# Retention's queries computed with channels on partitions, and the rotation tables moved: one change to a two-layer hybrid decoder kernel

## Chip, cores and metric

The kernel runs on one core of a Trainium2 chip. The metric is the device time of one execution in microseconds (us), as the median of several runs. A trace of one further execution shows when each engine was busy: PE (matmul), PEld (its weight loads), DVE (vector), ACT (scalar), POOL (GpSimd), and SP, which only issues DMAs here.

## The reference

Two layers of a decoder trunk over 1024 tokens and 1024 channels. Each layer norms and modulates its input, projects it to 3088 columns, and runs three groups of heads on them: attention over a window of 128, retention, and gated linear attention (GLA). Their outputs, gated, go through one output projection. Retention is what the change touches:

```python
rq = apply_rotary(rq.reshape(B, S, RET_HEADS, RET_DK), positions, ret_freq)
rk = apply_rotary(rk.reshape(B, S, RET_HEADS, RET_DK), positions, ret_freq)
r = retention(rq, rk, rv)          # 4 heads of 64, chunks of 128 tokens
# in a chunk: sc = (q k^T) * decay(i - j);  out = sc v + (q * q_decay) state
#             state = chunk_decay * state + (k * k_decay)^T v
r_out = rms_norm(r) * silu(rg)
```

`apply_rotary` multiplies the two halves x1 and x2 of each head by cosines and sines of position times frequency: (x1 cos - x2 sin, x2 cos + x1 sin). Attention and retention have different frequencies, so there are two sets of tables.

## The kernel before, in words

**Tiles.** Tokens stand in 8 tiles of 128, taken in pairs p = 0 to 3. The normed and transposed input of a pair, `hT`, holds channels on partitions, as a high and a low part; weights are split alike when they are loaded (ACT or DVE makes the high part, DVE or POOL the low part, L533). A projection of one tile is 24 products of 128x256: three combinations of parts over 8 slices of channels. `project` has the tokens as the stationary side, so its result has tokens on partitions; `project_T` has the weights as the stationary side, so its result has channels on partitions, and serves 512 tokens at once. Results go to three PSUM banks in turn (`mm`), everything else to five (`aux`).

**The order of the work.** PE's order is the order in which the program is written, and it is written with a clock: every matmul adds its estimated time to `clk`, jobs (Python generators) say how long to wait before their next step (the numbers in the table `L`), and after every 7 products `pump` runs the steps that are due. A flag with a delay does the same for a result that others await. So a number in `L` moves a step of a job between the products of a projection, on PE and, through the scheduler that follows program order, on the other engines. All DMAs but a few are issued by SP, in order: a DMA whose source isn't ready holds those behind it.

**Retention** (in `layer`, from L1500 on). For each pair the queries, keys and values of two tiles are projected, tokens on partitions. `ret_rot` rotates queries and keys on DVE with five instructions (`rotary`, L823 to L828) and multiplies them by a decay per token and head (L1157: `qdec`, `kdec`). Values are copied by ACT. `ret_core` then transposes queries and keys of a tile with four PE transposes into one bank, copies the bank to SBUF (ACT, 512 columns), makes scores of keys and queries (4 products of 64 rows, two banks), masks them on DVE (L1179), and multiplies them with the values and the state; DVE updates the state (L1198, L1200). The output is normed per head and gated (L973 to L979).

**Tables.** `tables` computes the sines and cosines of all tokens on DVE and ACT, tokens on partitions (L414 to L442, `sincos`). Retention uses them as they are. Attention has its queries with channels on partitions; for it `tables_T` repeats the sines over heads (DVE, L449), transposes (four PE transposes for each of 4 pairs), copies and stores to DRAM (`tabS`, L458), and `attn_rot` loads them back with 16 DMAs (L864).

**Banks and weights.** While a bank of `mm` is read by DVE or ACT, two more projections can run; the third needs it again. Weights of later units are loaded through 5 staging buffers (`st`) that they share with the modulation weights of the next layer; those are multiplied and summed on DVE (L364).

Of the kernel before, what the change touches and what calls it, by code (L numbers as in the profile page):

```python
# [60 lines left out]
def host_constants():  # L61
# [12 lines left out]
    c["qdec"] = (gam[None, :] ** (i[:, None] + 1.0)).astype(f)  # L74
    c["kdec"] = (0.125 * gam[None, :] ** (-(i[:, None] + 1.0))).astype(f)
# [18 lines left out]
def trunk(ctx: ExitStack, tc: tile.TileContext, ins, cst, out):  # L94
# [168 lines left out]
    tabS = dr.tile([NP_, P, 2, 256], F32, name="tabS")  # L263
# [147 lines left out]
    def tables():  # L411
        PIF = float(np.nextafter(np.float32(math.pi), np.float32(0)))
        ang = t2()
        V.tensor_tensor(ang.rearrange("p (t k) -> p t k", t=NT), posf.unsqueeze(2).to_broadcast((P, NT, 64)),  # L414
                        freq.unsqueeze(1).to_broadcast((P, NT, 64)), ALU.mult)
        yield
        nn = t2()
# [7 lines left out]
        n2 = t2()  # L425
# [4 lines left out]
        red = t2()  # L430
# [13 lines left out]
    def tables_T():  # L444

        for p in range(NP_):
            yield L["tt1"]
            rep_ = t2()
            V.tensor_copy(rep_.rearrange("p (s t h k) -> p s t h k", s=2, t=2, h=4),  # L449
                          sincos[:, 2 * p:2 * p + 2, :, 0:32].rearrange("p t s k -> p s t k").unsqueeze(3)  # L450
                          .to_broadcast((P, 2, 2, 4, 32)))
# [179 lines left out]

    def rstd_of(ss, w, scale, eps):
        r = small(w)
        V.tensor_scalar(r, ss, scale, eps, ALU.mult, ALU.add)  # L634
# [133 lines left out]
    qdec = cload("qdec")  # L768
    kdec = cload("kdec")
# [89 lines left out]
    def attn_rot(l, hf, g, w_):  # L859
# [3 lines left out]
        for s, d in ((0, sn), (1, cs)):  # L863
            nc.sync.dma_start(d.rearrange("p (s n) -> p s n", s=2),  # L864
                              tabS[2 * hf:2 * hf + 2, :, s, :].rearrange("s p n -> p s n"))
# [288 lines left out]
    def ret_rot(t, src, dec_):  # L1154
        r = t1()
        rotary(r, src, 4, t, 1)
        eng("rdec").tensor_tensor(h4(r), h4(r), dec_.unsqueeze(2).to_broadcast((P, 4, 64)), ALU.mult)  # L1157
# [564 lines left out]
```

## Time and profile before

| | before |
|---|---|
| median of 3 runs | 998.0 us (997.8 to 999.6) |
| the profiled execution's own time | 996.3 us |
| its span, first to last instruction | 994.6 us |
| instructions | 19641 |
| PE, DVE, ACT, POOL busy | 965.7, 683.2, 409.3, 246.3 us |
| retention, layer 1 and layer 2 | about 93 to 206 us and 593 to 677 us |
| PE's clock, mean | 0.991 of full |

The span is divided into busy time and idle time of each engine. Matmuls overlap: a product's time from start to end is longer than the distance between the starts of two neighbours, and it is the distance that adds up. The tables of groups name an engine's instructions by source line, output, input and shape; the last part of a group's row is the time for which the engine stood idle before them, and what it then waited for.

### The profile page before, as it was taken

The page shows a single profiled execution, that of the slowest core. Times are in us where ns is not written, and L with a number is a line of the kernel's source. Part 1 is how long each engine was busy: PE and PEld are TensorE (multiplying, and loading weights), DVE is VectorE, ACT ScalarE, POOL GpSimd, SP SyncE. Part 2 cuts the span into 40 slices and gives each one's busy share as a digit, 9 for nine tenths or more (in the row PEclk, how much of TensorE's full clock was granted, in tenths as well). Part 3 has the DMA queues.
Part 4 walks back from the last instruction along what each step waited for, and adds up shares of the span by engine and source line. Part 5 has one row for each costly group of instructions (what it writes and reads, how often), then busy time and mean ns, then how long its engine had stood idle before and what let it go on. Part 6 is the DMA issues. An engine that isn't in the chain of part 4 may idle for free.

```text
span 994.6 us, 19641 instructions
## 1 busy us (share of the span) xinstructions
PE 965.7 (97%) x7133; PEld 824.3 (83%) x7133; DVE 683.2 (69%) x1679; ACT 409.3 (41%) x1152; POOL 246.3 (25%) x310
## 2 busy tenths in 40 slices
PE   5899999999999999999999999999999999999996
PEld 1599999888998777778889999988999877777785
DVE  3779857677766777664677286775766577567876
ACT  2477312233332656632555332133333257574222
POOL 2322001233310234420124101113322034545000
PEclk8899999999999999999999999999999999999999
DMA  9843513523135355587555241352122434378883
GB/s 321 290 138 97 159 44 115 177 86 121 61 100 166 91 157 168 170 274 239 189 170 171 69 150 38 118 157 83 53 93 86 127 91 133 112 235 266 267 262 139
DMA packets 112305, 148.77 MB, mean 150 GB/s; under 512 B 12065, under 2 KB 63821, under 8 KB 112209
## 3 DMA queue, kind: packets, MB, share of 16 engines
q1 hardware_dynamic: 106512, 137.96, 44.5%
q10 hardware_dynamic: 5696, 9.56, 2.6%
q8 instruction: 56, 0.92, 0.4%
q14 instruction: 41, 0.33, 0.1%
HBM read 109.20 MB, written 36.18 MB: 146 GB/s over the span
## 4 chain that ended last, share of the span: by engine, by line
PE 80%; DVE 7%; DMA 7%; issue 2%; POOL 1%; ACT 1%; SPq 0%; ACTq 0%; POOLq 0%; DVEq 0%
PE mm L165 61%; PE aux L165 14%; PE aux L180 5%; DMA st<-in_w_in_dram 2%; POOL sm L635 1%; DMA t<-aoS 1%; DMA st<-in_w_last_dram 1%; DMA xk<-in_x_dram 1%; DVE arena L533 1%; DMA a<-mixS 1%; DVE t L1248 0%; DVE t L328 0%; DMA t<-in_x_dram 0%; DMA t<-xs 0%; DMA mixS<-t 0%
## 5 line engine op out<-in xcount | busy, mean ns | idle before, releaser
L165 PE MATMUL mm<-arena 128*128 128x256 f32 (+2 forms) x1824 | 299.9, 318 | 1.8 <-ACT arena L704 1.8
L165 PE MATMUL mm<-arena,arena 128*128 128x256 f32 (+2 forms) x1824 | 298.2, 316 | 0.0
L165 PEld LDWEIGHTS mm<-arena 128*128 128x128 f32 x1824 | 255.5, 191 | 26.0 <-issue 3.3
L165 PEld LDWEIGHTS mm<-arena,arena 128*128 128x128 f32 x1824 | 252.2, 188 | 24.3 <-issue 3.7
L635 POOL TENSOR_TENSOR sm<-sm,mhalf 128x1 f32<-128x1 f32 (+1 forms) x64 | 55.8, 872 | 335.9 <-DVE sm L634 317.8
L165 PE MATMUL mm<-arena,mx 128*128 128x512 f32 (+1 forms) x564 | 130.6, 387 | 0.5 <-ACT kept L1341 0.5
L165 PEld LDWEIGHTS mm<-arena,mx 128*128 128x128 f32 x564 | 101.4, 188 | 24.7 <-issue 1.9
L149 ACT ACTIVATE t<-aux 128x256 f32<-128x256 f32 (+2 forms) x124 | 55.8, 468 | 73.8 <-PE aux L180 62.2
L149 ACT ACTIVATE arena<-st 128x512 fp32r<-128x512 f32 x94 | 56.2, 627 | 53.2 <-DMA st<-in_w_in_dram 19.4
L929 POOL TENSOR_TENSOR smx<-smx,sm 128x512 f32<-128x512 f32 x32 | 36.1, 1129 | 125.7 <-DVE sm L928 118.0
L533 POOL TENSOR_TENSOR arena<-st,arena 128x512 fp32r<-128x512 f32 x31 | 42.7, 1378 | 79.7 <-ACT arena L149 72.9
L533 DVE TENSOR_TENSOR arena<-st,arena 128x512 fp32r<-128x512 f32 x77 | 58.0, 775 | 5.2 <-ACT arena L149 3.3
L925 ACT ACTIVATE smx<-smx,sm 128x129 f32<-128x129 f32 x128 | 49.9, 393 | 25.9 <-DVE sm L922 25.7
L364 DVE SCALAR_TENSOR_TENSOR acc<-st,c_act,acc 128x512 f32<-128x512 f32 x60 | 46.7, 778 | 16.9 <-DMA st<-in_w_mod_dram 16.5
L180 PE MATMUL aux<-c_ident,t 128*128 128x128 f32 (+1 forms) x292 | 48.2, 282 | 5.4 <-DVE t L666 5.0
L180 PEld LDWEIGHTS aux<-c_ident,t 128*128 128x128 f32 (+1 forms) x292 | 35.0, 144 | 12.4 <-DVE t L666 6.9
L698 ACT ACTIVATE t<-aux,mod,mod 128x128 f32<-128x128 f32 x68 | 25.9, 459 | 43.0 <-DVE t L1248 18.1
L165 PEld LDWEIGHTS aux<-t,mx 32*128 32x128 f32 (+1 forms) x896 | 39.5, 187 | 3.9 <-issue 2.1
L973 ACT ACTIVATE t<-aux 128x256 f32<-128x256 f32 x32 | 12.3, 383 | 73.6 <-PE aux L165 65.0
L165 PE MATMUL aux<-t,mx 32*128 32x32 f32 (+1 forms) x896 | 40.7, 272 | 0.0
L920 DVE COPY_PREDICATED smx<-c_curmask,aux 128x256 f32<-128x256 int32 x64 | 25.4, 446 | 19.5 <-ACT smx L149 17.2
L1248 DVE SCALAR_TENSOR_TENSOR t<-t,sm,t 128x512 f32<-128x512 f32 x32 | 24.0, 780 | 18.2 <-DMA t<-in_x_dram 10.8
(224 smaller groups left out, 1387.7 us busy)
## 6 DMA issues: line engine op xcount, KB each, us to landing
st<-in_w_in_dram SPq DMA_DIRECT2D x96, 256.0 KB, 3.8
st<-in_w_mod_dram SPq DMA_DIRECT2D x64, 256.0 KB, 3.1
mx<-mixS SPq DMA_DIRECT2D x20, 512.0 KB, 4.9
mixS<-t SPq DMA_DIRECT2D x72, 128.0 KB, 3.7
st<-in_w_last_dram SPq DMA_DIRECT2D x36, 256.0 KB, 3.8
wm<-in_w_mod_dram SPq DMA_DIRECT2D x12, 512.0 KB, 7.0
t<-in_x_dram SPq DMA_DIRECT2D x24, 256.0 KB, 4.9
t<-tabS SPq DMA_DIRECT2D x16, 256.0 KB, 4.6
```

What stands on the lines that cost most here:

```text
L149: A.activation(dst, src, AF.Copy)
L165: T.matmul(dst, lhsT, rhs, start=start, stop=stop)
L180: T.transpose(dst, src, idn)
L364: V.scalar_tensor_tensor(acc, wt, c_act[:, k:k + 1], acc, ALU.mult, ALU.add)
L533: e.tensor_tensor(lo, st, f(hi), ALU.subtract)
L635: G.tensor_tensor(r, r, mhalf[:, :w], ALU.pow)
L698: A.activation(hf[:, ks], at[kt], AF.Identity, scale=gain, bias=shift)
L920: V.copy_predicated(sv, curmask.unsqueeze(1).to_broadcast((P, 2, P)), pv[:, :, n // P - 1, :])
L925: A.activation(sm[:, h, :], sm[:, h, :], AF.Exp, bias=mx[:, h:h + 1], accum_out=sums[:, h:h + 1])
L929: eng("pn").tensor_tensor(sm[:, :, 0:128], sm[:, :, 0:128], rs.unsqueeze(2).to_broadcast((P, 4, P)), ALU.mult)
L973: A.activation(sq, po, AF.Square)
L1248: V.scalar_tensor_tensor(xt[j], yg[j], r, xt[j], ALU.mult, ALU.add)
```

## The change

**Queries.** `ret_q` projects the queries of a pair with the weights as the stationary side, 2 x 24 products of 128x256 into one bank, channels on partitions, and rotates them there with six DVE instructions on 512 columns: four partial products with the sines, each on 32 partitions and written to the neighbouring 32, one product with the cosines, one sum. Queries are kept for the pair in `rq`, and need no transposes. A group of 32 partitions is one half of one head.

**Decays.** They leave queries and keys. Values are multiplied by `vdec` on DVE, straight from PSUM, instead of being copied by ACT; the query's factor is left out, since the norm per head removes it, but for its constant: `reps` has a value per token and head.

**Tables.** `sincos` is transposed as it is, 8 PE transposes in all. The two halves are stored to `tabS`; four loads put retention's part into SBUF for good (`tab`, one copy for each group of 32 partitions), and 16 stores of 32 partitions write attention's part, once for each of 4 heads, to `tabA`, from which `attn_rot` loads. The computation of the tables uses a large buffer in place of small ones and is due earlier (`tb1` 12.59 instead of 24.5), and the first queries await the flag `tab`.

**Copies and masks.** The copy of the transposed keys (256 columns now) and the masking of scores are put at high priority for the scheduler.

**Delays.** Some 40 numbers of `L` are changed, and four are new.

```diff
+    tabS = dr.tile([2, 2, 32, S], F32, name="tabS")
+    tabA = dr.tile([4, 32, 2, S], F32, name="tabA")
+    tab = cp.tile([P, 2, S], F32, name="tab")
...
     def tables_T():
-        for p in range(NP_):
-            yield L["tt1"]
-            rep_ = t2()
-            V.tensor_copy(rep_..., sincos[:, 2 * p:2 * p + 2, :, 0:32]...)
-            yield L["tt2"]
+        for i in range(2):
+            yield L["tt1"] if i == 0 else L["tt2"]
             pt = aux()
-            for i in range(4):
-                transp(pt[:, i * P:(i + 1) * P], rep_[:, i * P:(i + 1) * P], ident)
+            for t in range(4):
+                transp(pt[:, t * P:(t + 1) * P], sincos[:, 4 * i + t].rearrange("p s k -> p (s k)"), ident)
             tb = t2()
             A.activation(tb, pt, AF.Copy, scale=0.125)
-            nc.sync.dma_start(tabS[p], tb.rearrange("p (s n) -> p s n", s=2))
+            ts = slice(512 * i, 512 * i + 512)
+            nc.sync.dma_start(tabS[:, :, :, ts].rearrange("s c k n -> (s c k) n"), tb)
+            tbs.append(tb)
+        yield L["tt3"]
+        for b in range(4):
+            nc.sync.dma_start(tab[32 * b:32 * b + 32], tabS[:, 1].rearrange("s k n -> k s n"))
+        flag("tab", L["tt6"])
+        for i in range(2):
+            for h in range(4):
+                yield L["tt4"]
+                for j in range(2):
+                    nc.sync.dma_start(tabA[h, :, j, 512 * i:512 * i + 512], tbs[i][64 * j:64 * j + 32])
...
+    def project_P(pm, l, p, w, c):
+        h = hT[(l, p)]
+        accum(pm, lambda a, k: w[:, a, k, c:c + P], lambda b, k: h[:, b, k, 0:256])
...
+    def ret_q(l, p, w):
+        pm = mm()
+        for c in range(2):
+            project_P(pm[:, 256 * c:256 * c + 256], l, p, w, c * P)
...
+        for b in range(4):
+            r = slice(32 * b, 32 * b + 32)
+            o = two(x)[32 * (b ^ 1):32 * (b ^ 1) + 32]
+            if b % 2:
+                V.scalar_tensor_tensor(o, two(pm)[r], -1.0, sn[r], ALU.mult, ALU.mult)
+            else:
+                V.tensor_tensor(o, two(pm)[r], sn[r], ALU.mult)
+        V.tensor_tensor(two(u), two(pm), cs, ALU.mult)
...
+        V.tensor_tensor(q, u, x, ALU.add)
+        flag(("rq", l, p), L["rq1"])
...
     def ret_core(l, t, q, k, v):
...
         for j in range(2):
-            transp(pt[:, j * P:(j + 1) * P], q[:, j * P:(j + 1) * P], ident)
-            transp(pt[:, (2 + j) * P:(3 + j) * P], k[:, j * P:(j + 1) * P], ident)
-        copy("rT", tt_, pt)
+            transp(pt[:, j * P:(j + 1) * P], k[:, j * P:(j + 1) * P], ident)
+        kTt = t1()
+        with tc.high_priority():
+            copy("rT", kTt, pt[:, 0:256])
+        yield (0.0, ("rq", l, t // 2))
...
-                        copy("rv", v, src)
+                        V.tensor_tensor(h4(v), h4(src), vdec.unsqueeze(2).to_broadcast((P, 4, 64)), ALU.mult)
...
-"rc1": 0.8, "rc1@1": 0.37, "rc3@1": 1.9, "tb1": 24.5, "tb2": 0.75, "pf2": 4.16, "kv2": 2.11
+"rc1": 0.8, "rc1@1": 0.0, "rc3@1": 2.72, "tb1": 12.59, "tb2": 0.89, "pf2": 5.11, "kv2": 5.4
```

The order of instructions, at three places. PE, layer 1, from the first value projections (`mm`) of pair 0 to the first scores; before:

```order
L165 MATMUL mm_1428<-arena_320,arena_71 128x256 x24
L165 MATMUL mm_1458<-arena_320,arena_71 128x256 x7
L165 MATMUL aux_1466<-gaT_417,gwt 128x512
L180 MATMUL aux_1476<-c_ident,t_222_1281 128x128
L180 MATMUL aux_1476<-c_ident,t_234_1368 128x128
L180 MATMUL aux_1476<-c_ident,t_222_1281 128x128
L180 MATMUL aux_1476<-c_ident,t_234_1368 128x128
L165 MATMUL mm_1458<-arena_320,arena_71 128x256 x14
L165 MATMUL aux_1497<-t_251_1481 128x128
```

And in the changed kernel, where `rq` holds the queries and t_241 the transposed keys:

```order
L165 MATMUL mm_1433<-arena_322,arena_71 128x256 x24
L165 MATMUL mm_1463<-arena_322,arena_71 128x256 x14
L180 MATMUL aux_1478<-c_ident,t_230_1385 128x128 x2
L165 MATMUL mm_1463<-arena_322,arena_71 128x256 x7
L165 MATMUL aux_1490<-gaT_419,gwt 128x512
L165 MATMUL mm_1463<-arena_322,arena_71 128x256 x3
L165 MATMUL aux_1508<-rq_1345,t_241_1481 128x128
```

Two transposes of keys are left of four, and 10 products with a gate's product stand between them and the scores, where 14 did.

DVE, the same place, from the first rotation on; before, the first query rotation (`mm_1206`) and what follows it:

```order
L823 TENSOR_TENSOR t_222_1281<-mm_1206,sincos 128x256
L1066 TENSOR_TENSOR gs_1249<-gs_1249,t_216_1235 128x2
L825 TENSOR_TENSOR tr_1282<-mm_1206,sincos 128x4x32
L826 TENSOR_TENSOR tr_1282<-mm_1206,sincos 128x4x32
L827 TENSOR_TENSOR t_222_1281<-t_222_1281,tr_1282 128x4x32
L828 TENSOR_TENSOR t_222_1281<-t_222_1281,tr_1282 128x4x32
L449 COPY t_237_1384<-sincos 128x512
L1157 TENSOR_TENSOR t_222_1281<-t_222_1281,c_qdec 128x256
```

In the changed kernel the query product of the pair is `mm_1231`, the first key product `mm_1351`:

```order
L1184 TENSOR_TENSOR t_224_1339<-mm_1231,tab 32x512
L1182 SCALAR_TENSOR_TENSOR t_224_1339<-mm_1231,tab 32x512
L1184 TENSOR_TENSOR t_224_1339<-mm_1231,tab 32x512
L838 TENSOR_TENSOR t_230_1385<-mm_1351,sincos 128x256
L840 TENSOR_TENSOR tr_1386<-mm_1351,sincos 128x4x32
L841 TENSOR_TENSOR tr_1386<-mm_1351,sincos 128x4x32
L1182 SCALAR_TENSOR_TENSOR t_224_1339<-mm_1231,tab 32x512
L1185 TENSOR_TENSOR t_223_1338<-mm_1231,tab 128x512
```

Three more of this rotation and the five of the second key tile follow, and behind these the value weights (`st` of L154, as `arena_322`), with the modulation's (`acc`) between them:

```order
L843 TENSOR_TENSOR t_234_1424<-t_234_1424,tr_1425 128x4x32
L541 TENSOR_TENSOR arena_322<-st_1321,arena_322 128x512
L366 SCALAR_TENSOR_TENSOR acc_1244<-st_1332,c_act,acc_1244 128x512
L541 TENSOR_TENSOR arena_322<-st_1349,arena_322 128x512
L366 SCALAR_TENSOR_TENSOR acc_1244<-st_1402,c_act,acc_1244 128x512
```

The six instructions of a pair's rotation replace ten and two decays of the two tiles, and the low parts of the value weights come after the second key rotation.

SP, between the stores of gates (`sgS`, `srS`) at the end of layer 1's gate projections, in the changed kernel; before, no table was handled here:

```order
L460 DMA tab<-tabS 32x2x1024
L154 DMA sgS<-t_191_1111 128x256
L460 DMA tab<-tabS 32x2x1024 x3
L154 DMA sgS<-t_197_1155 128x256
L154 DMA srS<-t_202_1191 128x256
L466 DMA tabA<-t_178_1047 32x512 x2
L154 DMA srS<-t_206_1227 128x256
L466 DMA tabA<-t_183_1085 32x512 x4
L154 DMA st_1321<-in_w_in_dram 128x512
L466 DMA tabA<-t_183_1085 32x512 x2
```

The loads of `tab` and ten of the small stores stand between the gates' stores and the value weights.

More of the change, by code (lines that the diff above doesn't have):

```diff
@@ L1500, in layer @@
         G.memset(stR, 0.0)
-        await_flag("tables")
+        await_flag("tab")
         for p in range(NP_):
             last = p == NP_ - 1
-            rr = {}
-            for name in ("rq", "rk", "rv"):
+            q = ret_q(l, p, used(l, "rq"))
+            pump()
+            if last:
+                load(l, "gqk")
+            ks = {}
+            for name in ("rk", "rv"):
                 w = used(l, name)
```

71 lines of the change are left out of this document (38 added, 33 removed).

## The prediction

> **What bounds the kernel now.** I read the page's engine line and slices first, then the table by stretches for the two places where retention runs, then the tensor engine's waits, and last its timeline for the price of one transpose.
>
> ```profile
> PE 965.7 (97%) x7133; PEld 824.3 (83%) x7133; DVE 683.2 (69%) x1679; ACT 409.3 (41%) x1152; POOL 246.3 (25%) x310
> PE   5899999999999999999999999999999999999996
> PE 80%; DVE 7%; DMA 7%; issue 2%; POOL 1%; ACT 1%; SPq 0%; ACTq 0%; POOLq 0%; DVEq 0%
> 93.00:206.00 113.00, 111.71 (x908) 106.39 (x908) 80.08 (x232) 31.22 (x67) 18.39 (x18) 1.00 0.40 122
> 593.00:677.00 84.00, 81.58 (x671) 77.50 (x670) 56.30 (x167) 21.27 (x45) 12.03 (x12) 1.00 0.34 105
> ```
>
> PE is busy nearly everywhere between the first and the last slice, and it is 80% of the chain that ended last. In the two stretches of retention (columns: length, busy time of PE, weight loads, DVE, ACT, POOL, then PE's clock) it is short of full by 1.3 and 2.4 us; DVE has 71% and 67%. So an instruction less on PE there is time less, if nothing else becomes late. What PE waits for there:
>
> ```profile
> PE aux L165 <- ACT t L149: 3.0, 3, 1.3
> PE aux L165 <- DVE t L1179: 0.4, 1, 0.4
> PE aux L165 <- DVE stR L1200: 0.3, 1, 0.3
> 192.83 0.71 PE L165 MATMUL aux<-t 64*128 64x128 f32 x8 [1.29 <-ACT t L149]
> 669.66 0.71 PE L165 MATMUL aux<-t 64*128 64x128 f32 x8 [1.22 <-ACT t L149]
> ```
>
> The 3.0 us are score products that wait for ACT's copy of the transposed queries and keys; with the two other rows it is 3.7 us, the whole of what these stretches wait.
>
> **Term 1: transposes go.** In each of 16 retention tiles (8 per layer) four transposes become two, and the tables need 8 instead of 16.
>
> ```profile
> 158.69 0.38 PE L180 MATMUL aux<-c_ident,t 128*128 128x128 f32 x2
> 158.83 3.11 PE L165 MATMUL mm<-arena 128*128 128x256 f32 x24
> 161.78 0.60 PE L180 MATMUL aux<-c_ident,t 128*128 128x128 f32 x4
> 162.13 2.28 PE L165 MATMUL mm<-arena 128*128 128x256 f32 x17
> L180 PE MATMUL aux<-c_ident,t 128*128 128x128 f32 x288 | 47.5, 283 | 5.4 <-DVE t L666 5.0 <-DVE mx L1121 0.2
> ```
>
> From start to start, a block of two holds PE for 0.14 us (158.69 to 158.83) and one of four for 0.35 (161.78 to 162.13): 0.21 for the two that go. 16 x 0.21 = 3.4, and two blocks of four for the tables are 0.7: **-4.1 us**. The group's mean of 283 ns is the time of one from start to end, and neighbours overlap; by it the 40 would be 11.3 us, the far end. The query product itself keeps its size: 48 products of 128x256 for two tiles before and after, only with the weights as the stationary side, as the rest of the kernel already has it in other stages.
>
> The Trainium skill, page "TensorE: Matmul & The Clock Gate", section "Part 4: PE-mode transpose", gives about 275 ns for a transpose inside a kernel; by that figure the 40 would be worth an estimated 11 us, against 4.1 by the starts. The trace has that number as the mean of one, 283 ns, and not as the spacing.
>
> **Term 2: the copy that PE waits for is halved.**
>
> ```profile
> L149 ACT ACTIVATE t<-aux 128x512 f32<-128x512 f32 x48 | 28.6, 595 | 25.7 <-PE aux L180 22.4 <-DVE t L1602 2.5 <-issue 0.4
> L149 ACT ACTIVATE t<-aux 128x256 f32<-128x256 f32 x44 | 16.8, 382 | 26.0 <-PE aux L180 17.6 <-PE aux L165 7.0 <-POOL arena L533 1.3
> ```
>
> 595 ns become 382, so the three waits lose 0.2 us each, 0.6 to 0.7. ACT also loses the 16 copies of values (one is moved to DVE below). The copy is put at high priority, but in the new order of ACT a conversion of weights, which waits for its DMA, still stands one or two instructions ahead of it at the last tile of each layer, so I don't credit the whole 3.0 us. Between 0 and -3.0 I take **-0.7**.
>
> **Term 3: DVE pays for the new form.** Old and new prices come from these rows.
>
> ```profile
> 599.48 0.41 DVE L823 TENSOR_TENSOR t<-mm,sincos 128x256 f32<-128x256 f32 x1
> 599.81 0.28 DVE L825 TENSOR_TENSOR tr<-mm,sincos 128x128 f32<-128x128 f32 x1
> 600.01 0.28 DVE L826 TENSOR_TENSOR tr<-mm,sincos 128x128 f32<-128x128 f32 x1
> L378 DVE TENSOR_TENSOR modg<-aux,st 128x512 f32<-128x512 f32 x4 | 2.7, 684 | 0.2 <-PE aux L165 0.2
> L364 DVE SCALAR_TENSOR_TENSOR acc<-st,c_act,acc 128x512 f32<-128x512 f32 x60 | 46.7, 778 | 16.9 <-DMA st<-in_w_mod_dram 16.5
> 595.97 0.57 DVE L1198 TENSOR_TENSOR stR<-stR,aux 64x128 f32<-64x128 f32 x2
> L825 DVE TENSOR_TENSOR tr<-mm,sincos 128x128 f32<-128x128 f32 x32 | 8.9, 278 | 0.0
> L1198 DVE TENSOR_TENSOR stR<-stR,aux 64x128 f32<-64x128 f32 x28 | 7.9, 281 | 0.2
> ```
>
> Rotating one tile took 0.33 + 4 x 0.20 = 1.13 us from start to start and the decay 0.33 more: for queries and keys of two tiles 4 x 1.46 = 5.8. Fewer partitions don't make an instruction shorter: 64 partitions take 281 ns (L1198) where 128 take 278 (L825). So each of the four partial multiplications, on 32 partitions of 512, costs what a whole one costs: 0.68 as a plain product, 0.78 with the sign; the cosine product and the sum are two more of 0.68. Together 4.3 us if nothing overlaps and 3.8 if each gives up the 0.08 that whole ones do. The keys (2 x 1.13) and the values (2 x 0.33, which stood on ACT) are 2.9. That is 6.7 to 7.2 for two tiles instead of 5.8, or at most 1.4 x 8 = 11 us of DVE over the kernel. In stretches where DVE has 29 to 33% free this hides; its price, if the cover were gone, is the rival "bank" below.
>
> The Trainium skill, page "VectorE: DVE Perf Modes", section "Two Vector instructions with no wait between them", says that an instruction is held until all earlier ones are finished when its start quadrant of 32 partitions differs from the last one's. By that rule the upper value, 4.3, is right, by plain overlap 3.8. The two L1198, on different halves, agree: 0.57 for two that follow each other, where L825 and L826 start 0.20 apart.
>
> **Term 4: the first queries push the value weights.** In layer 1 the second and third low part of the value weights (L541) stand in DVE's new order behind the first query rotation and both key rotations; before, they were done between the rotations. Call X the end of the first query product. A product of 24 takes 2.95 us (158.83 to 161.78), so the two key products end at X+2.95 and X+5.9, and the value product wants the second part at its 18th instruction and the third at its 20th: X+8.1 and X+8.3. DVE, in its order: three partial rotations to X+2.2, three instructions of the first key rotation from X+2.95 to X+3.7, the rest of both to X+6.2; the second key rotation to X+7.3; the second part, a 128x512 product of 0.7, to X+8.0 (in time), a weight of the modulation 0.78 (L364), the third part to X+9.5, or X+8.9 where the whole ones overlap. PE waits 0.6 to 1.2 us, once: I take **+0.9**. In layer 2 these weights stand ahead of the rotation. The bounds are 0 and 2.
>
> **Term 5: tables earlier, and out and in through DRAM.** Each is hidden, but narrowly enough to be told.
>
> ```profile
> 50.00:100.00 50.00, 50.00 (x415) 49.73 (x414) 43.73 (x106) 37.24 (x95) 12.08 (x24) 1.00 0.39 119
> 48.84 1.36 DVE L700 TENSOR_SCALAR t<-aux,mod,mod 128x128 f32<-128x128 f32 x4 [0.19 <-PE aux L180]
> 60.75 0.88 DVE L666 TENSOR_SCALAR t<-t,sm 128x512 f32<-128x512 f32 x2 [0.73 <-DMA st<-in_w_in_dram]
> 82.85 1.04 DVE L700 TENSOR_SCALAR t<-aux,mod,mod 128x128 f32<-128x128 f32 x3
> 83.86 1.04 PE L165 MATMUL mm<-arena,arena 128*128 128x272 f32 x7
> 84.41 1.28 DVE L708 TENSOR_TENSOR arena<-t,arena 128x512 fp32r<-128x512 f32 x2
> 92.27 0.43 DVE L442 TENSOR_SCALAR sincos<-sincos 128x512 f32<-128x512 f32 x1
> mixS<-t SPq DMA_DIRECT2D x16, 256.0 KB, 3.5
> t<-tabS SPq DMA_DIRECT2D x16, 256.0 KB, 4.6
> t<-t SPq DMA_DIRECT2D x32, 64.0 KB, 2.0
> ```
>
> PE now transposes the finished table just before the end of its 12th projection, which is 83.5 us in before (the 13th starts at 83.86); before, the table was ready at 92.7. DVE therefore does the 16 table instructions between the preparations of tiles 4 to 6 instead of after them. Both orders are at the same instruction at 48.84. From there to the last table instruction the new one has 20 of L700 (0.32 apart), 9 of L708 (0.60), 9 gates of 256 columns (0.33, as L823), 4 pairs of L666 (0.80), 3 weight differences and a cast (2.2), ten table instructions like L708 and six like L442 (8.1), and small ones (1.3): 29.5 us, thus 78.4 with no wait, and 82.6 if DVE rests 13% of the time, as in 50 to 100 before; I take 81, since table work fills part of the rests. PE comes at 83.5: nothing, but with 2 us in hand. Then copy 0.6, store 3.5, SP's queue and four loads (1 MB in four, 4.6 and 1.2 for the issues behind each other): 10 us, while PE has 27 instructions of 272 columns and 96 of 256 in front of the end of the first query product, some 15 us. Hidden by 5. The 16 stores of 64 KB stand on SP between weights, some 0.35 us of the queue each; the weights behind them come up to 3 us later, and are wanted later still. The 16 loads for attention keep their bytes. **0 us**, at worst +3.
>
> **The sum.** -4.1 - 0.7 + 0.9 = -3.9. The profiled execution took 996.3 us, of which 994.6 are its span; that gives 992.4. The median of the runs shown is 998.0, 1.7 above it, so I predict **994.0**.
>
> **Rivals.**
>
> *Cancelled by the start.* If DVE is some 2 us slower through the preparation of tiles 4 to 7 than I add up, PE stands at the table's transposes and again at tile 7, and every later thing shifts: 2 to 4 us, so 996 to 998. Against it is DVE's slack above; for it, that DVE's rests are few there. Chance 0.14.
>
> *Bank, the slower side.* Products go to three banks. The query product's bank is read by five DVE instructions and is wanted again after two key products, 5.9 us after it was filled. DVE needs 4.3 with what stands between; once it starts 1.6 us late, PE waits at the first value product. If state updates and modulation weights (0.78 each) put it 2.8 us late, this costs 1.2 at all eight pairs, 9.6: 1003.6. Against it is DVE's free 30%, for it that DVE works in order and its waits for POOL and DMA stand in the same queue. Chance 0.16.
>
> *Waits vanish.* The copy is early at all three places and the new delays leave no other wait in retention: -4.1 - 3.7 = -7.8, 990.2. The delays are the same mechanism: they set the distance between transposes and scores. Chance 0.17.
>
> *Transposes worth their mean.* 283 ns each: -11.3 - 0.7 + 0.9, so 986.9. The starts speak against it. Chance 0.03. By the Trainium skill's page "TensorE: Matmul & The Clock Gate", section "Part 4: PE-mode transpose", this is the case to expect.
>
> The forecast itself, 992 to 996, has 0.50.
>
> **Range and chances.** Only some 0.2% (2 us) can be told from no change. Faster than 996.0: 0.50 + 0.17 + 0.03 = 0.70, same 0.14, slower 0.16. The range leaves out the far transposes and the worst of the bank: 988.5 to 1000.5. The likeliest case alone would be 992 to 996.
>
> **What would show it.** Right: PE's busy time some 4 us less, transposes in blocks of two before the scores, the waits for ACT's copy at or under 2.4 us, a wait at the first value product of layer 1 of about 1 us for L541. Wrong: PE idle at the transposes of the table or at the projection of tile 7 (start); idle before value products with DVE's rotation as the releaser (bank); the first query rotation waiting for the load of the table (DRAM).

## The result, and the profile after

| | before | changed |
|---|---|---|
| median of 22 runs | 997.46 us | 997.23 us |
| lowest to highest | 994.9 to 1001.7 | 991.9 to 1000.5 |
| ratio, 95% interval | | 0.9995 (0.9984 to 1.0006) |
| profiled execution, its span | 996.31, 994.6 | 991.94, 990.2 |

The change makes no difference that can be measured; 994.0 was forecast. The profiled execution of the changed kernel is the fastest of its 22. One execution differs from the next by some us in the first 70 us and in how long PE ran at half clock, so I took a second trace of it (996.33 us); its first projection starts at 37.55 us, where that of before starts at 37.73, and stretches of these two can be compared.

The engine lines of the page, first and second trace of the changed kernel:

```profile
PE 960.9 (97%) x7093; PEld 820.6 (83%) x7093; DVE 693.7 (70%) x1627; ACT 399.5 (40%) x1135; POOL 244.6 (25%) x310
```

```profile
PE 963.7 (97%) x7093; PEld 820.8 (83%) x7093; DVE 693.9 (70%) x1627; ACT 398.8 (40%) x1135; POOL 247.7 (25%) x310
```

DVE's busy time rose by 10.5 to 10.7 us, about as added up; PE's fell by 2.0 to 4.8. But idle time came back. To see where, I cut the span at the same products in each trace: the kernels have the same 4332 projection products, and those numbered 201, 1201, 2641 and 3361 bound three stretches: layer 1 from its last input tiles to the end of its retention and part of GLA, a middle part, and layer 2 from its gates to the end of its retention and part of GLA. The table of stretches (length, PE busy, weight loads, DVE, ACT, POOL, PE's clock), before:

```profile
71.15:250.27 179.12, 177.41 (x1582) 167.21 (x1581) 137.56 (x384) 63.83 (x153) 37.77 (x48) 1.00 0.37 113
250.27:576.32 326.05, 325.75 (x2234) 274.06 (x2233) 211.75 (x485) 151.13 (x449) 82.85 (x109) 1.00 0.50 156
576.32:707.19 130.87, 128.45 (x1110) 120.68 (x1109) 89.19 (x267) 34.46 (x82) 22.28 (x27) 1.00 0.32 99
```

The changed kernel, second trace (the first has 181.09, 325.56 and 129.13):

```profile
70.96:251.63 180.67, 176.86 (x1557) 165.11 (x1556) 138.76 (x348) 58.39 (x143) 39.78 (x50) 1.00 0.42 126
251.63:577.22 325.59, 325.59 (x2234) 274.10 (x2233) 213.50 (x491) 150.30 (x449) 81.74 (x108) 1.00 0.49 154
577.22:706.34 129.12, 126.67 (x1093) 118.87 (x1092) 93.77 (x238) 30.00 (x74) 23.34 (x27) 1.00 0.34 105
```

**Layer 2 gains 1.75 us**, all in PE's busy time (128.45 to 126.67), which is what 16 transposes should give; its idle time, 2.4, stays, though every wait in it is a new one. **Layer 1 loses 1.6 to 2.0 us**, where 24 transposes fewer should give 2.5: PE's idle time rises from 1.7 to 3.8. The rows of PE's waits that bear on these stretches, from the whole second trace of the changed kernel (us in total, times, longest):

```profile
PE mm L165 <- ACT arena L719: 2.4, 2, 1.8
PE mm L165 <- ACT arena L149: 1.8, 2, 1.6
PE mm L165 <- DVE t L1185: 1.3, 1, 1.3
PE aux L165 <- DVE sm L649: 1.1, 1, 1.1
PE mm L165 <- DVE t L1006: 0.5, 1, 0.5
PE aux L165 <- DVE stR L1241: 0.5, 1, 0.5
```

The three waits for ACT's copy, 3.0 us before, are gone altogether. Over the three stretches PE's idle time rises from 4.4 us to 6.3, and its busy time falls by only 2.5, so that 0.7 us is left. In their place stand 1.8 us for ACT's conversion of weights, 1.3 for the rotation that reads a bank (L1185), 1.1 for the norm of a head, 0.6 (the shorter one for L719; the 1.8 stood in before too) and 0.5 while layer 1's last tiles are projected, and 0.5 for the state.

The largest is at layer 1's first value products, in PE's timeline of the second trace:

```profile
110.93 0.50 PE L165 MATMUL mm<-arena,arena 128*128 128x256 f32 x2 [0.20 <-ACT arena L149]
113.05 4.06 PE L165 MATMUL mm<-arena,arena 128*128 128x256 f32 x32 [1.61 <-ACT arena L149]
```

ACT in turn waits for the loads (its timeline, same trace):

```profile
107.78 0.63 ACT L149 ACTIVATE arena<-st 128x512 fp32r<-128x512 f32 x1 [2.02 <-DMA st<-in_w_in_dram]
110.25 0.63 ACT L149 ACTIVATE arena<-st 128x512 fp32r<-128x512 f32 x1 [1.83 <-DMA st<-in_w_in_dram]
112.36 0.63 ACT L149 ACTIVATE arena<-st 128x512 fp32r<-128x512 f32 x1 [1.48 <-DMA st<-in_w_in_dram]
```

And SP issues these loads late. Its timeline before, where the four loads of the value weights are out by 96.7 us:

```profile
89.78 2.21 SPq L154 DMA_DIRECT2D st<-in_w_in_dram  x2
95.16 0.34 SPq L154 DMA_DIRECT2D st<-in_w_in_dram  x1
96.32 0.33 SPq L154 DMA_DIRECT2D st<-in_w_in_dram  x1
```

In the changed kernel, second trace, three of them stand behind and between the stores of attention's tables:

```profile
98.14 0.93 SPq L466 DMA_DIRECT2D tabA<-t  x2
100.47 0.34 SPq L154 DMA_DIRECT2D srS<-t  x1
100.85 3.02 SPq L466 DMA_DIRECT2D tabA<-t  x4
103.91 0.43 SPq L154 DMA_DIRECT2D st<-in_w_in_dram  x1
104.39 0.92 SPq L466 DMA_DIRECT2D tabA<-t  x2
106.65 0.38 SPq L154 DMA_DIRECT2D st<-in_w_in_dram  x1
107.08 0.90 SPq L466 DMA_DIRECT2D tabA<-t  x2
108.02 0.42 SPq L154 DMA_DIRECT2D st<-in_w_in_dram  x1
```

### The profile page after: what moved, and what is told of

Same layout as the page of the kernel before. It is cut to its first block, busy times and chain, and to the rows that moved or that the text cites. A ratio compares the mean times of both kernels' runs of the same rounds, so it can differ in the third digit from the quotient of the medians.

```text
span 990.2 us, 19487 instructions
## 1 busy us (share of the span) xinstructions
PE 960.9 (97%) x7093; PEld 820.6 (83%) x7093; DVE 693.7 (70%) x1627; ACT 399.5 (40%) x1135; POOL 244.6 (25%) x310
## 4 chain that ended last, share of the span: by engine, by line
PE 83%; DVE 9%; DMA 3%; issue 2%; ACT 1%; POOL 1%; ACTq 0%; POOLq 0%; DVEq 0%; SPq 0%
PE mm L165 63%; PE aux L165 16%; PE aux L180 4%; DMA st<-in_w_mod_dram 1%; DMA xk<-in_x_dram 1%; DVE acc L366 1%; DVE arena L541 1%; POOL sm L650 1%; DMA st<-in_w_in_dram 1%; DVE t L1182 0%; DVE t L330 0%; DVE t L681 0%; DVE t L1184 0%; DVE t L1073 0%; DVE t L1185 0%
## 5 line engine op out<-in xcount | busy, mean ns | idle before, releaser
L149 ACT ACTIVATE t<-aux 128x256 f32<-128x256 f32 (+2 forms) x124 | 51.8, 438 | 98.0 <-PE aux L180 75.6
L943 POOL TENSOR_TENSOR smx<-smx,sm 128x512 f32<-128x512 f32 x32 | 35.7, 1116 | 129.1 <-DVE sm L942 116.9
L541 POOL TENSOR_TENSOR arena<-st,arena 128x512 fp32r<-128x512 f32 x31 | 42.6, 1376 | 93.2 <-ACT arena L149 74.4
L541 DVE TENSOR_TENSOR arena<-st,arena 128x512 fp32r<-128x512 f32 x77 | 58.2, 775 | 2.4 <-ACT arena L149 0.9
L180 PE MATMUL aux<-c_ident,t 128*128 128x128 f32 (+1 forms) x244 | 40.9, 280 | 6.4 <-DVE t L681 4.8
L180 PEld LDWEIGHTS aux<-c_ident,t 128*128 128x128 f32 (+1 forms) x244 | 29.4, 143 | 13.1 <-DVE t L681 6.2
```

What stands on the lines that cost most here:

```text
L149: A.activation(dst, src, AF.Copy)
L180: T.transpose(dst, src, idn)
L541: e.tensor_tensor(lo, st, f(hi), ALU.subtract)
L943: eng("pn").tensor_tensor(sm[:, :, 0:128], sm[:, :, 0:128], rs.unsqueeze(2).to_broadcast((P, 4, P)), ALU.mult)
```

## The experiments

Theory A: the transposes' time is gained as predicted, and lost again in new waits, above all in layer 1: the value weights behind the table's stores, a bank in layer 2, the projections at the start. Its rivals: the gain never was one (retention is paced by something else than PE's time, or the second profile is the rule and PE's busy time did not fall), or the new delays give it back.

The table has all kernels. "At full clock" is the mean over the runs of time x mean granted clock: what is left when half of all time at half clock is counted as lost. It is a rough measure (half clock behind the last product costs nothing), but for the kernel before it is steady, 987.9 to 988.0 in four sets of 11 to 29 runs, from which its row has these two columns. The last three columns are the lengths of the stretches in the one trace of each.

| kernel | median us (runs) | to before, 95% interval | clock | at full clock | layer 1 | middle | layer 2 |
|---|---|---|---|---|---|---|---|
| before | 997.5 (22) | | 0.990 | 988.0 | 179.1 | 326.1 | 130.9 |
| changed | 997.2 (22) | 0.9984 to 1.0006 | 0.990 | 987.2 | 181.1 | 325.6 | 129.1 |
| again | 996.5 (12) | 0.9967 to 1.0000 | 0.991 | 987.1 | 180.7 | 325.6 | 129.1 |
| keys_only | 1002.3 (10) | 1.0033 to 1.0071 | 0.984 | 986.9 | 177.9 | 331.9 | 130.2 |
| keys_same_order | 994.9 (12) | 0.9961 to 0.9988 | 0.990 | 984.9 | 179.6 | 328.1 | 128.7 |
| four_transposes | 1009.3 (6) | 1.0092 to 1.0133 | 0.986 | 995.8 | 190.5 | 325.7 | 132.3 |
| four_same_order | 1003.2 (6) | 1.0052 to 1.0078 | 0.990 | 993.6 | 186.7 | 325.6 | 131.4 |
| old_delays | 1004.2 (11) | 1.0059 to 1.0121 | 0.985 | 991.1 | 184.8 | 327.3 | 129.5 |
| tabA_later | 992.6 (5) | 0.9950 to 0.9974 | 0.991 | 984.2 | 179.4 | 325.6 | 128.7 |
| tabA_actq | 994.5 (12) | 0.9962 to 0.9985 | 0.991 | 986.0 | 180.7 | 325.6 | 128.5 |
| act_copies | 1001.9 (6) | 1.0036 to 1.0062 | 0.988 | 989.3 | 187.5 | 325.6 | 128.3 |
| short_tables | 995.1 (12) | 0.9974 to 0.9998 | 0.992 | 987.2 | 181.2 | 325.6 | 128.6 |
| mod_behind | 993.4 (12) | 0.9949 to 0.9974 | 0.991 | 984.8 | 179.4 | 325.6 | 127.1 |
| low_on_pool | 991.3 (6) | 0.9924 to 0.9950 | 0.991 | 982.8 | 179.3 | 325.6 | 127.3 |

### again

No edit.

> The changed kernel once more, for a second trace. Theory A (the transposes' 4 us are gained and then given back in new waits, mostly ahead of and in layer 1's retention): PE's busy time again 4 to 5 us under that of the kernel before, PE's idle time between 50 and 200 us again 1 to 3 us above it, and the time within 0.2% of it. Theory B (the give-back in the one profile is chance, the gain is real): 993 to 994 us. Theory C (PE's busy time never fell, the profile's 960.9 is chance): PE busy 964 us or more.

996.5 us, so theory B falls: the two traces agree within 0.4 us in each stretch, and the give-back in layer 1 is no chance. PE's busy time over the whole span, 963.7, lies between A's number and C's and decides nothing, since it grows with the time at half clock in the first 50 us. In the three stretches together PE was busy 631.6 us before and 629.1 in both traces after, so it did fall, by 2.5, and C falls too.

### keys_only, four_transposes: the first tries

```diff
-            transp(pt[:, j * P:(j + 1) * P], q[:, j * P:(j + 1) * P], ident)
-            transp(pt[:, (2 + j) * P:(3 + j) * P], k[:, j * P:(j + 1) * P], ident)
+            transp(pt[:, j * P:(j + 1) * P], k[:, j * P:(j + 1) * P], ident)
...
-        copy("rT", tt_, pt)
+        copy("rT", qT, pt[:, 0:256])     # qT also stands for kTt
```

> The kernel before without the 32 transposes of queries; the scores and the carried state take the transposed keys in the queries' place, and everything else stays, the rotation of the queries too. This is terms 1 and 2 alone. Theory A (the transposes stood on the path at 0.105 us each, and the copy that PE waits for is shorter): 3.4 to 4.1 us faster than the kernel before. Theory D (retention's steps are paced by their fixed places between the products and not by PE's time): within 1 us of the kernel before. By the mean of 283 ns: 9 us faster.

```diff
+        for j in range(2):
+            transp(pt[:, (2 + j) * P:(3 + j) * P], k[:, j * P:(j + 1) * P], ident)
```

> The changed kernel with two idle transposes put back into each of the 16 retention tiles, behind the two that it has; nobody reads them, and the copy stays at 256 columns. Theory A: 3.4 us slower than the changed kernel. Theory D: within 1 us of it. By the mean of 283 ns: 9 us slower.

Neither theory's number came: the first is 4.8 us slower than before, the second 12 to 13 slower than the changed kernel. Both edits also move the planner's clock, which adds 0.109 us for each transpose, and so move other jobs between products. The first one's trace has a stretch of 10 us at half clock in its middle part (331.9 instead of 326.1), and its loss is one of clock: at full clock it is 1.1 us faster than before. So neither run tests the transposes alone; the next pair holds the planner's clock.

### four_same_order

```diff
+        for j in range(2):
+            T.transpose(pt[:, (2 + j) * P:(3 + j) * P], k[:, j * P:(j + 1) * P], ident)   # clk stays
```

> The changed kernel with two idle transposes per retention tile, as in the run before, but with the planner's clock not advanced for them, so that the order of PE's other instructions stays as it is. Theory A (0.105 us each on PE's path, and the 12.8 us of the last such run came from jobs that the planner moved): 3.4 us slower than the changed kernel. If a transpose costs its mean of 283 ns: 9 us slower. If the moved jobs were not the cause: again 12 us slower. If retention's steps are paced by other things: within 1 us.

6 us slower than the changed kernel, which is neither 3.4 nor 9. The trace splits it. In layer 2, 16 transposes more cost 1.80 us of PE (126.67 to 128.47), **0.112 each**, which for 32 is 3.6. Most of the rest, in this one trace, is a wait in layer 1 that the changed kernel hasn't, and half clock behind it. PE's timeline of this kernel:

```profile
197.63 1.13 PE L165 MATMUL aux<-rq,t 64*128 64x128 f32 x8 [2.79 <-ACT t L149]
```

ACT's order has changed by one row: a conversion of weights, waiting for its load, now stands ahead of the copy of the keys.

```profile
196.68 0.63 ACT L149 ACTIVATE arena<-st 128x512 fp32r<-128x512 f32 x1 [3.21 <-DMA st<-in_w_in_dram]
197.22 0.37 ACT L149 ACTIVATE t<-aux 128x256 f32<-128x256 f32 x1
```

So theory A's price holds in PE's busy time, though not its forecast of the whole; the mean of 283 ns is refuted, and so is the theory that retention is paced by other things.

### keys_same_order

```diff
+            clk[0] += 0.109     # in keys_only, for each transpose left out
```

> The kernel before without the 32 transposes of queries (the scores and the carried state take the transposed keys in their place), with the planner's clock still advanced for them, so that PE's other instructions stand where they stood. Theory A: 3.4 us faster by the transposes and 0 to 1 more by the shorter copy, so 993 to 994 where the kernel before has 997.5; the waits for ACT's copy, 3.0 us, fall to about 2.4. If the copy's wait only takes up the time that PE saves: within 1 us of the kernel before, and the waits for the copy grow.

994.9 us, 2.2 below before and a little above the 993 to 994 expected; at full clock it is 3.1 below. In layer 2 PE's busy time falls by 1.8 (128.45 to 126.66), 0.112 for each of 16; the waits for the copy are 2.8 instead of 3.0. So **the transposes are worth 3.1 to 3.6 us in the old kernel too**, and the shorter copy, by these waits, 0.2, under the 0.7 of term 2. The median shows less; in the trace the difference stands in the middle part (328.1 instead of 326.1, most of it new waits) and in 3.4 us at half clock behind a wait of 1.64 us in layer 1.

### old_delays

The table `L` of before in the changed kernel, but for `tt`, `tb` and `rq1`.

> The changed kernel with the delays of before for all jobs but the tables (their start, their steps, their loads and stores) and the queries' flag, which the kernel before has not. If the new delays give back the gain: 2 to 4 us faster than the changed kernel. If they brought the gain and the rest gives it back: 1 to 4 us slower. If delays of this size only trade one short wait for another: within 1 us.

7 us slower than the changed kernel: the second case (the new delays brought the gain), beyond its range. At full clock it is 4 us, the rest is clock. Layer 1 is 3.7 to 4.1 us longer: PE waits 1.5 us for the finished table at its transposes and 1.0 behind them. The delays are part of the change's value, and do not give it back.

### tabA_later and tabA_actq

```diff
-                yield L["tt4"]
+                yield L["tt4"] if i or h else 14.0
```

> The changed kernel with the 16 stores of attention's tables begun 14 us later on the planner's clock. In SyncE's order the last three loads of layer 1's value weights then stand ahead of 10 of the stores instead of behind 12 to 16 of them; PE's and ACT's orders are the same. If the stores on that queue cause the wait at the first value products (1.9 us idle at 110 to 113 us of the span, in both traces of the changed kernel): the three loads land 3 us or more earlier, that idle time falls under 1 us, what is left is DVE's part behind the rotations, and the time falls by 1 to 1.5 us. If DVE's order alone causes it (term 4): the idle time stays at 1.5 us or more, and the time too.

In its own trace SP issues the three loads at 99.03 and 100.05, and of the wait only DVE's part is left:

```profile
99.03 0.43 SPq L154 DMA_DIRECT2D st<-in_w_in_dram  x1
99.56 0.40 SPq L154 DMA_DIRECT2D st<-in_w_mod_dram  x1
100.05 0.85 SPq L154 DMA_DIRECT2D st<-in_w_in_dram  x2
```

```profile
111.63 2.40 PE L165 MATMUL mm<-arena,arena 128*128 128x256 f32 x18 [0.81 <-DVE arena L541]
```

992.6 us, 4 to 4.7 below the changed kernel and more than expected; layer 1 is 1.3 to 1.7 us shorter, layer 2 0.5, at full clock it is 2.9. Then the same stores on ACT's queue:

```diff
-                    nc.sync.dma_start(tabA[h, :, j, ...], tbs[i][64 * j:64 * j + 32])
+                    A.dma_start(tabA[h, :, j, ...], tbs[i][64 * j:64 * j + 32])
```

> The changed kernel with the 16 stores of attention's tables issued by ACT instead of SyncE, at their old place in the plan; PE's order is the same. Their bytes and their moment stay, only SyncE's queue is rid of them. Theory queue (they hold up the value weights that stand behind them on SyncE): the idle time at the first value products falls from 1.9 us to under 1 us as in the run with later stores, and the time to 992 to 995. Theory traffic (the 1 MB in small packets slows the weights' transfers wherever it is issued): the idle time stays and the time is within 1 us of the changed kernel's 996.5 to 997.2.

994.5 us. The waits at the value products are 0.3 and 0.6, with 0.3 more a product earlier, so 1.2 instead of 1.8; the loads are issued less early, since the loads of `tab` now hold SP's queue themselves. By its time theory queue has it, by its waits half; layer 1 is not shorter in its one trace. The first run shows that the value weights pay for the place of these stores on SP, and the second that more than the stores stands there.

### act_copies and mod_behind: the bank

The 1.3 us in layer 2 have this origin (DVE's timeline, second trace of the changed kernel; the query product ended at 580.3):

```profile
581.19 2.57 DVE L366 SCALAR_TENSOR_TENSOR acc<-st,c_act,acc 128x512 f32<-128x512 f32 x2
583.79 0.68 DVE L1184 TENSOR_TENSOR t<-mm,tab 32x512 f32<-32x512 f32 x1
584.48 0.68 DVE L1182 SCALAR_TENSOR_TENSOR t<-mm,tab 32x512 f32<-32x512 f32 x1
585.18 0.69 DVE L1184 TENSOR_TENSOR t<-mm,tab 32x512 f32<-32x512 f32 x1
585.88 0.69 DVE L1182 SCALAR_TENSOR_TENSOR t<-mm,tab 32x512 f32<-32x512 f32 x1
586.59 0.69 DVE L1185 TENSOR_TENSOR t<-mm,tab 128x512 f32<-128x512 f32 x1
```

```profile
587.43 3.11 PE L165 MATMUL mm<-arena 128*128 128x256 f32 x24 [1.32 <-DVE t L1185]
```

The two modulation products at 581.19 take 2.57 us together, though DVE is not idle before either. The first alone took 1.78, while GpSimd made a low part of weights beside it (DVE's and POOL's timelines, same trace):

```profile
581.19 1.78 DVE L366 SCALAR_TENSOR_TENSOR acc<-st,c_act,acc 128x512 f32<-128x512 f32 x1
580.72 1.71 POOL L541 TENSOR_TENSOR arena<-st,arena 128x512 fp32r<-128x512 f32 x1 [5.64 <-ACT arena L149]
```

The first run lets ACT copy the bank:

```diff
-        u, x = t2(), t2()
+        u, x, sb = t2(), t2(), t2()
+        A.activation(sb, pm, AF.Copy)
+        pm = sb
```

> The changed kernel with ACT copying each pair's query product out of its bank (128x512, eight copies more of 0.6 us), and DVE rotating the copy; PE's order is the same. Theory bank (DVE's rotation holds the bank, once, in layer 2's first pair): PE's wait of 1.3 us with the cosine product as its releaser goes, no other wait of that kind comes, and the time falls by 1.3 us. If the wait is DVE's being late altogether and moves to the next thing that DVE owes: the idle time stays near 1.3 us under another name, and the time within 0.5 us.

The wait for L1185 goes, but in the same pair PE waits 0.9 us for the key's rotation (L843): DVE was late altogether, as the second theory had it. What made the kernel 5 us slower stands in layer 1 (187.5 us instead of 180.7): ACT's order moved with the new copies, and the copy of the keys came behind a conversion again, 2.6 us; PE waited 2.2 us for the state (L1243, 0.5 in the changed kernel), which DVE did behind a rotation; and 3.4 us ran at half clock.

```profile
200.89 0.71 PE L165 MATMUL aux<-rq,t 64*128 64x128 f32 x8 [2.62 <-ACT t L149]
596.32 0.44 PE L180 MATMUL aux<-c_ident,t 128*128 128x128 f32 x2 [0.93 <-DVE t L843]
```

Then DVE's order instead (with the later stores):

```diff
+                    with tc.issue_after(rot[0].ins):     # layer 2: L366 behind L1185
                         V.scalar_tensor_tensor(acc, wt, c_act[:, k:k + 1], acc, ALU.mult, ALU.add)
...
-        job(mod_all(l, (2,)))
+        if l == 0:
+            job(mod_all(l, (2,)))
...
             q = ret_q(l, p, used(l, "rq"))
+            if l and p == 0:
+                job(mod_all(l, (2,)))
```

So layer 2's modulation job also starts later, behind the first query product.

> The kernel with the later stores (992.6), and in layer 2 the modulation's products put behind the first query rotation in DVE's order, which stood two of them ahead of it, one waiting for its weights. If that lateness of DVE is the whole of the bank's wait: the 1.4 us of PE ahead of the second key product of layer 2 go, and the time falls by 1.4 us to 991. If DVE is late anyway, another wait of 1 us or more comes in that pair, and the time stays within 0.5 us of 992.6.

The rotation starts at 579.95, half a microsecond behind the product's end, and the wait is gone; layer 2 is 1.6 us shorter in the trace:

```profile
585.10 3.04 PE L165 MATMUL mm<-arena 128*128 128x256 f32 x24
```

The median is 993.4 with 12 runs from 990.1 to 997.1, and does not show it against the five of tabA_later. That the two modulation products ahead of the rotation make the wait is shown; that one of them waits for its load, as the expectation has it, is not what the second trace shows, nor that of tabA_later, where they take 0.74 and 0.75 us at 579.19 and 579.97 with no idle time between them. The worth in time is not shown either.

### short_tables

```diff
         for i, cv in enumerate(cw_consts(1.0)):
-            V.scalar_tensor_tensor(red, n2, -cv, red if i else ang, ALU.mult, ALU.add)
+            if i == 0:
+                V.scalar_tensor_tensor(red, n2, -cv, red if i else ang, ALU.mult, ALU.add)
             yield
```

> The changed kernel without three of the four steps that bring the angles near zero a second time; the sines are then less exact. DVE has three instructions of 0.68 us less between 66 and 78 us, where PE projects tiles 4 to 7. Theory start (DVE's table work now stands between the preparations of tiles, and makes PE wait twice, 0.6 and 0.5 us at 74 and 81 us): both waits go, DVE ends the table 2 us earlier, and the time falls by 1 us. If those waits come from ACT's or the weights' side: they stay, and the time too.

Both waits stay, 0.6 and 0.7 us, and at full clock nothing is gained: these three instructions of DVE's table work do not make them. That the median is 1.4 to 2 us below that of the changed kernel is in the clock, 0.992 against 0.990 to 0.991, which the edit has no part in that I can see. What makes PE wait at these two products stays open. A lead that no run tests: some 5 us ahead of the first wait one of DVE's low parts took 1.79 us instead of 0.68 in this trace and in the second one of the changed kernel (at 70.50), both times beside GpSimd, and in the trace of before none did.

### low_on_pool

```diff
-                e = G if first == 0 or name[0] == "o" and kc == 2 else eng(f"wlo{kc}")
+                e = G if first == 0 or name[0] == "o" and kc == 2 or l == 0 and name == "rv" else eng(f"wlo{kc}")
```

> The kernel with the later stores and the modulation behind the rotation (993.4), and the three low parts of layer 1's value weights that DVE makes given to GpSimd (1.4 us each there instead of 0.7). PE's, ACT's and SyncE's orders are the same. If term 4 is right (they stand on DVE behind the first rotations): PE's wait of 0.9 us at the first value products with that low part as its releaser goes, DVE is 2 us freer there, and the time falls by 0.5 to 1 us, to 992.5. If their input or the slower engine sets it: the wait stays, under GpSimd's name, and the time is within 0.3 us of 993.4.

On mod_behind. The first value products run through without a wait:

```profile
110.99 4.66 PE L165 MATMUL mm<-arena,arena 128*128 128x256 f32 x38
```

991.3 us (0.9924 to 0.9950 of before), the fastest of all, 5 to 6 us below the changed kernel. Its trace gives the 0.9 back at two later waits of layer 1, so term 4's cause is shown, but its worth only as part of the three edits together: at full clock 4.4 us below the changed kernel, in the three stretches 3.3 to 3.7.

## Where the prediction was right and where wrong, step by step

**What came.** 997.2 lies in the range, but the range reached from 9.5 us under the 998.0 of before to 2.5 over it and held "no change" too, so that says little for the forecast; its own 992 to 996 did not come. The time is that of "cancelled by the start"; its mechanism is only a part of the cause. In place of -4.1 - 0.7 + 0.9 the three stretches of the second trace show -4.0 for the transposes, +1.5 for PE's other instructions and +1.8 for its waits (4.4 gone, 3.0 of them for the copy, and 6.3 come), which leaves -0.7.

**Term 1 was right.** 0.112 us for each transpose, in both kernels, against 0.105; with 32 of them gone and 8 fewer for the tables, 40 x 0.112 is 4.5. Added up from start to start over both layers, the transposes took 4.0 us less in the second trace. The far rival, 283 ns each, is out: it is the duration of one, not the distance between two. The group after has the same duration with 48 fewer of it on record (32, and the tables' 16, whose 8 new ones read `sincos` and are not in this row):

```profile
L180 PE MATMUL aux<-c_ident,t 128*128 128x128 f32 x240 | 40.0, 281 | 5.8 <-DVE t L681 5.1 <-ACT t L1119 0.4 <-DVE mx L1135 0.2
```

**Term 2 reached its far bound,** for a reason I had doubted. The waits for the copy did not shrink by 0.7, they went, 3.0 us: in ACT's new order the conversion just ahead of the copy had its load in time (192.40 us in the second trace, the copy 193.20, the scores 194.13), and those whose loads came later stand behind it. keys_same_order shows that the halved copy itself is worth 0.2. How thin this is, four_same_order and act_copies show: one row in ACT's order brings back 2.8 and 2.6 us. So "waits vanish" came true for the old waits, but not its condition that no new ones come; low_on_pool, with three new ones removed, has 991.3, near its 990.2.

**Term 3 was right.** DVE took 10.5 us more ("at most 11"); of this 1.75 stands in the middle part, where nothing was changed, and the clean figure is layer 2's, 4.6 for four pairs (89.2 to 93.8), 1.15 each, inside the 0.9 to 1.4 added up. The partial products cost what whole ones cost and do not overlap: 0.69 to 0.71 from start to start in the rows above, where 0.61 lies between the cosine product and the next (586.59 and, from the same view, 587.20).

```profile
L1182 DVE SCALAR_TENSOR_TENSOR t<-mm,tab 32x512 f32<-32x512 f32 x16 | 11.0, 689 | 0.3
L1184 DVE TENSOR_TENSOR t<-mm,tab 32x512 f32<-32x512 f32 x16 | 11.0, 685 | 4.5 <-PE mm L165 4.2
```

The Trainium skill, page "VectorE: DVE Perf Modes", section "Two Vector instructions with no wait between them", has the hold for instructions of different start quadrants; the trace agrees, with 0.08 to 0.10 us each. The sign cost nothing here (689 and 685 ns), where I had put 0.1. Its price, the rival **bank**, came once in eight pairs and not in all: DVE began 3.5 us late, PE stood 1.3 us.

**Term 4 was right**, 0.8 us in the first trace for the 0.9 of the sum; in the second it hides behind the conversion that comes later still.

**Term 5 failed, and with it the forecast.** The step: "The 16 stores of 64 KB stand on SP between weights, some 0.35 us of the queue each; the weights behind them come up to 3 us later, and are wanted later still." The issue of a store took 0.43 us in the median, up to 1.9, and with the table's other transfers and the stores of gates between them, the last three loads of the value weights were issued at 103.9 to 108.0 instead of 91.7 to 96.3: some 12 us later, not up to 3. They were wanted at 110, and PE waited 1.8 us. I had looked for the wait of the first queries for the table, and let the weights on the same queue pass with a sentence. Its other part, PE standing at tile 7 and the table's transposes, came as 0.6 and 0.5 us at the last tiles, and three instructions less of the table work that I blamed did not shorten them (short_tables). So a term put at 0 cost 2.9 us, near its "at worst +3". The bank's 1.3 us had its rival; the 1.1 for the norm of a head stood in no term.

**What is left open.** In layer 1 PE's other instructions took 1.9 us more, spread over scores (0.5), state and products. The 0.5 stands in one block of scores, at 169.25 in the second trace (1.27 us for eight, where others take 0.71); it goes on just as DVE ends a masking (L1220), so it looks like a short wait that counts as busy. For the rest I have no cause. And the sum of single effects in the traces (3.3 to 3.7 us for the three repairs) is less than the medians show (5 to 6); a part of the difference is the clock. The changed kernel is also built with `dynamic_dma_scratch_size=1024`, which no run here tests.

## What to carry to other kernels

Sum a removed instruction by the distance between starts; then look at what now comes last on every queue that the change adds to, for that decides whether the sum arrives. A DMA that nobody awaits still delays what stands behind it on its issuing engine: for each added transfer, name the next load behind it and when that is wanted. Where a program's order follows from a planner's clock, test an edit with that clock held, or the experiment measures the new order.

## What the runs showed of the hardware

A wait of PE could cost more than its length. In four_same_order the 2.79 us up to 197.63 are followed by half clock (PE's clock is the third number from the end):

```profile
193.40:196.80 3.40, 1.44 (x7) 0.81 (x5) 0.72 (x2) 0.19 (x2) 1.17 (x1) 1.00 0.88 284
196.80:200.20 3.40, 2.56 (x12) 2.05 (x13) 2.74 (x6) 1.89 (x4) 1.28 (x1) 0.64 0.61 191
200.20:203.60 3.40, 3.40 (x23) 3.08 (x22) 0.00 (x0) 0.34 (x1) 0.00 (x0) 0.85 0.89 305
```

The same came in act_copies behind a wait of 1.93 us, in keys_same_order behind one of 1.64 and in old_delays around two of 1.50 and 0.96, but not behind 1.61 in the second trace of the changed kernel or 2.62 in act_copies. The Trainium skill, page "TensorE: Matmul & The Clock Gate", section "Part 1: The HAM clock gate (the "warmup" mystery)", gives half speed after an idle window of about 3.4 us; here shorter waits sufficed at times, and each half-clock stretch between the first 50 us and the last product lasted 3.4 us or a multiple. In keys_only 10 us at half clock stand behind a wait of only 0.7 us, and are most of its loss.

An instruction of DVE could take much longer beside a busy GpSimd. In the second trace of the changed kernel 52 instructions of DVE took over 0.4 us more than the median of their group (those of one line, tile and shape, where there are four or more), and all 52 ran while POOL was busy, which is only 25% of the span; in the trace of before it is 43 of 43. An example (DVE's and POOL's timelines, second trace; other L541 of this shape take 0.68):

```profile
70.50 1.79 DVE L541 TENSOR_TENSOR arena<-st,arena 128x512 fp32r<-128x512 f32 x1
70.33 1.42 POOL L541 TENSOR_TENSOR arena<-st,arena 128x512 fp32r<-128x512 f32 x1 [0.66 <-ACT arena L149]
```

It is not so each time: in mod_behind the products of a rotation took their usual 0.68 to 0.69 beside a low part on POOL (579.23 to 581.06). What decides it no run shows.
